# Attention scores over the full 128 rows, and the order of every engine written down block by block

## The chip, the cores and the metric

The kernel runs on one core of one Trainium2 chip. The metric is device time in microseconds, taken over a whole execution of the program; the times given are medians over several executions, and lower is better. A core has five engines with a queue each: PE (TensorE, matrix products; PEld is its loading of weights), DVE (VectorE), ACT (ScalarE), POOL (GpSimd) and SP (SyncE, which issues transfers). Each takes its own queue in order, and they wait for one another by semaphores.

## The reference

One inference step of a two-layer network. 128 context tokens ("prompt") and 512 noisy tokens on an 8 by 64 grid ("sample") pass through an even layer (a pooling mixer beside a neighbourhood attention) and an odd layer (convolutions). The change lies in the even layer's attention, with 8 heads of 64:

```python
s_loc = jnp.einsum('brqhd,brkwhd->bhrqkw', qg, k_band).astype(jnp.float32) * scale + bias
s_loc = jnp.where(col_ok[:, None, :], s_loc, -jnp.inf)
s_ctx = jnp.einsum('brqhd,bhld->bhrql', qg, kc).astype(jnp.float32) * scale
s = jnp.concatenate([s_loc.reshape(bsz, N_HEADS_B, rows, GRID_W, n_loc), s_ctx], axis=-1)
p = jax.nn.softmax(s, axis=-1).astype(v.dtype)
...
o = (jnp.einsum('bhrqkw,brkwhd->brqhd', p_loc, v_band)
     + jnp.einsum('bhrql,bhld->brqhd', p_ctx, vc))
```

Every sample query sees a band of 16 columns over all 8 rows, with a learned bias by relative position, and 128 cached context keys, in one softmax. The prompt's queries see the prompt's keys (`context_attention`, a plain softmax). Then the attention is gated by silu(g_b), and it goes with the pooling mixer through one output projection. Beside it, layer modulation needs `silu(cond) @ w_mod`, 3 by 1024 columns for each layer and for two conditions.

## The kernel before

Activations lie with channels on the 128 partitions and 640 tokens along the free dimension: 256 of the sample, 128 of the prompt, 256 of the sample. A projection takes a weight tile of 1024 by 128 (512 KB) and makes 128 output channels. Each float32 operand is split into a high part that the fast matmul takes exactly and a low rest (`split`: ACT copies the high part, DVE subtracts), and three products hi hi, hi lo and lo hi are added up in PSUM. `mm_k` issues the six matmuls of one slice of 128 input channels (three products, 384 and 256 tokens each); eight of them make one tile (`mtile`). Weight tiles come in the order of the list `order`; `next_w` and `ahead` load and split them up to two tiles ahead, from the queue of ACT.

The attention stage follows the projection to v (L532). For each of four pairs of heads (`attention(i)`) it projects k, then q, and splits both. The two heads of a pair lie on partitions 0 to 63 and 64 to 127. A block is 128 queries (8 columns by 8 rows, two groups of 8 columns; the edges form the fourth block) by 384 keys. For each of four blocks `scores` issues six matmuls: three products for each head, each over the 64 rows of that head (L587). Then `softmax`: DVE adds the bias and takes the minimum of the negated sum out of PSUM (L593), ACT makes the exponential and its sum (L596), DVE the reciprocal (L598) and the normalised row (L599). `flip` transposes the result on PE (L605) and ACT copies it out (L607); `values` multiplies by v (L617) into the bank `ps_o`. The prompt has its own scores (L628) and values (L651). Last come the gating (L675 to L682) and a split to `o_hi`, `o_lo`.

POOL builds the bias of each head out of `raw_b` (`build_bias`: L450 adds a mask, L452 copies, L454 makes two edge parts); `raw_b` holds all eight heads and is loaded from SP in 16 transfers (L518) during the pooling mixer. The rest of the modulation, 32 rows of 1024 columns in `todo`, is made on DVE: `fill_mod(n)` takes n rows, each with two products over 1024 elements (L260), and `dma_wt` issues the row for the next fill from SP (L251), with two buffers `wt`. How many rows are filled where is set by `FILL`, `FILL_P`, `FILL_V` and `FILL_O`. Two output tiles (`early`) are projected at the end of the stage.

What sets the order: in most of the program a planner places the instructions by its own costs and due times. `keep_in_program_order` ties one instruction to its place, `chain` ties the attention's matmuls to one another, and inside `manual_schedule(engines=...)` the engines named follow the order of the code; before, only the start of the program is written so. PSUM has eight banks: two tiles `mm` of two banks, two of `ps_s`, one each of `ps_t` and `ps_o`.

## Time and profile before

| | |
|---|---|
| time, median of 3 runs | 594.07 us (593.48 to 594.58) |
| span of the profiled execution, first to last instruction | 592.7 us |
| a time of its own for the profiled execution | not given; the median lies 1.4 us above its span |
| PE busy | 580.5 us, 98% |
| DVE busy | 444.2 us, 75% |
| ACT busy | 224.2 us, 38% |
| POOL busy | 39.1 us, 7% |
| granted TensorE clock, mean | 0.997 |

The profile lists one execution. A row of the order of time gives start and duration in us, engine, line, operation, output and inputs, shape and count, and in square brackets the idle time ahead of it with what ended that. A group row gives busy us, mean ns of one, and idle time before. Matmuls are pipelined: what one costs is the time from its start to the next one's start, not its duration. The chain of waits is followed back from the last instruction to whatever released each one.

### The profile page before, as it was taken

What the parts mean: (1) busy time and instruction counts of PE and PEld (TensorE: products, weight loads), DVE (VectorE), ACT (ScalarE), POOL (GpSimd) and SP (SyncE); (2) the same over time, 40 slices, a digit from 0 to 9 for tenths busy, and PEclk for the clock granted to TensorE, in tenths of its full rate; (3) what the DMA queues carried; (4) which work ended last, traced back from release to release, by engine and by line L of the source; (5) the groups of instructions that cost most, each with busy time, mean ns of one, the idle gap of its engine ahead of it and who ended that gap; (6) DMA issues with size and microseconds to landing.
All of it is one profiled execution on the core that took longest, in us unless ns stands there. A gap on an engine that the chain in (4) does not pass through costs nothing.

```text
span 592.7 us, 10405 instructions
## 1 busy us (share of the span) xinstructions
PE 580.5 (98%) x4218; PEld 538.7 (91%) x4218; DVE 444.2 (75%) x802; ACT 224.2 (38%) x392; POOL 39.1 (7%) x89
## 2 busy tenths in 40 slices
PE   9799999999999999999999999999999999999995
PEld 5699999988988788878999999999999999999994
DVE  0566577698979879775638889999999995457536
ACT  6557222223354555464325431123222222445220
POOL 1000000330004223100000000000000000000000
PEclk9999999999999999999999999999999999999998
DMA  8985566556833333311811232222222222110204
GB/s 306 373 361 173 175 177 173 149 191 204 270 96 128 108 111 102 118 71 43 273 41 37 72 115 88 83 72 72 72 71 72 74 84 91 53 57 2 72 0 178
DMA packets 24991, 74.21 MB, mean 125 GB/s; under 512 B 2800, under 2 KB 7024, under 8 KB 24816
## 3 DMA queue, kind: packets, MB, share of 16 engines
q1 hardware_dynamic: 15584, 39.86, 20.0%
q10 hardware_dynamic: 9360, 33.69, 17.2%
q8 instruction: 33, 0.54, 0.4%
q14 instruction: 14, 0.11, 0.1%
HBM read 70.39 MB, written 3.15 MB: 124 GB/s over the span
## 4 chain that ended last, share of the span: by engine, by line
PE 96%; DMA 1%; DVE 1%; ACT 0%; issue 0%; POOL 0%; DVEq 0%; SPq 0%; ACTq 0%; POOLq 0%
PE mm L162 77%; PE ps_o L617 3%; PE ps_s L587 3%; PE ps_t L605 3%; PE ps_s L532 2%; PE mm L301 2%; PE modacc L324 1%; DMA wm<-in_w_mod 1%; PE ps_t L532 1%; PE ps_o L532 1%; PE mm L532 1%; PE bc L200 1%; PE mm L494 1%; PE modtr L192 1%; PE stat L192 0%; DVE y L957 0%
## 5 line engine op out<-in xcount | busy, mean ns | idle before, releaser
L162 PE MATMUL mm<-h_lo,w_hi 128*128 128x384 f32 (+1 forms) x768 | 181.1, 311 | 0.5 <-DVE h_lo L345 0.5
L162 PE MATMUL mm<-h_hi,w_hi 128*128 128x384 f32 (+1 forms) x768 | 181.3, 313 | 0.0
L162 PE MATMUL mm<-h_hi,w_lo 128*128 128x384 f32 (+1 forms) x768 | 181.2, 311 | 0.0
L112 ACT CAST w_hi<-w_raw 128x1024 fp32r<-128x1024 f32 x68 | 70.9, 1054 | 162.9 <-PE mm L162 142.0
L162 PEld LDWEIGHTS mm<-h_hi,w_hi 128*128 128x128 f32 x768 | 119.1, 188 | 3.3 <-issue 2.1
L162 PEld LDWEIGHTS mm<-h_lo,w_hi 128*128 128x128 f32 x768 | 119.4, 188 | 2.5 <-issue 1.4
L162 PEld LDWEIGHTS mm<-h_hi,w_lo 128*128 128x128 f32 x768 | 119.5, 188 | 1.1 <-issue 1.1
L910 DVE SCALAR_TENSOR_TENSOR cv<-gl,small,cv 128x656 f32<-128x656 f32 x120 | 101.5, 901 | 0.4
L115 DVE TENSOR_TENSOR w_lo<-w_raw,w_hi 128x1024 fp32r<-128x1024 f32 x68 | 83.5, 1230 | 15.7 <-ACT w_hi L112 15.6
L260 DVE SCALAR_TENSOR_TENSOR junk<-wt,condb 128x1024 bf16<-128x1024 f32 x64 | 78.6, 1229 | 5.5 <-DMA wt<-in_w_modT 4.8
L162 PE MATMUL mm<-o_lo,w_hi 128*128 128x384 f32 (+1 forms) x256 | 67.8, 312 | 0.0
L162 PE MATMUL mm<-o_hi,w_lo 128*128 128x384 f32 (+1 forms) x256 | 67.7, 311 | 0.0
L162 PE MATMUL mm<-o_hi,w_hi 128*128 128x384 f32 (+1 forms) x256 | 66.7, 313 | 0.0
L162 PEld LDWEIGHTS mm<-o_hi,w_hi 128*128 128x128 f32 x256 | 43.0, 189 | 1.0 <-issue 0.6
L162 PEld LDWEIGHTS mm<-o_lo,w_hi 128*128 128x128 f32 x256 | 43.2, 189 | 0.8 <-issue 0.3
L162 PEld LDWEIGHTS mm<-o_hi,w_lo 128*128 128x128 f32 x256 | 43.2, 189 | 0.7 <-issue 0.5
L607 ACT COPY pt<-ps_t 128x384 f32<-128x384 f32 (+1 forms) x36 | 16.7, 464 | 24.4 <-PE ps_t L605 24.2
L596 ACT ACTIVATE sn<-sn,mx 128x384 f32<-128x384 f32 x32 | 19.6, 615 | 12.6 <-DVE mx L593 11.6
L593 DVE CUSTOM_DVE_ANT_0 sn<-ps_s,bias 128x384 f32<-128x384 f32 x32 | 17.2, 551 | 5.4 <-PE ps_s L587 5.3
L733 DVE SCALAR_TENSOR_TENSOR x<-mm,mod,x 128x128 f32<-128x128 f32 (+2 forms) x19 | 8.5, 494 | 14.8 <-PE mm L162 14.8
L733 DVE SCALAR_TENSOR_TENSOR x<-mm,mod,xre 128x128 f32<-128x128 f32 (+2 forms) x19 | 8.6, 493 | 14.3 <-PE mm L162 14.3
L605 PE MATMUL ps_t<-ident,sn 128*128 128x128 f32 x104 | 18.6, 285 | 0.5 <-ACT pt L607 0.3
(199 smaller groups left out, 601.4 us busy)
## 6 DMA issues: line engine op xcount, KB each, us to landing
wt<-in_w_modT SPq DMA_DIRECT2D x32, 512.0 KB, 4.2
w_raw<-in_w_in_odd ACTq DMA_DIRECT2D x28, 512.0 KB, 3.4
wm<-in_w_mod SPq DMA_DIRECT2D x16, 512.0 KB, 8.9
w_raw<-in_w_in_even ACTq DMA_DIRECT2D x16, 512.0 KB, 4.0
w_raw<-in_w_out_even ACTq DMA_DIRECT2D x8, 512.0 KB, 5.3
w_raw<-in_w_out_odd ACTq DMA_DIRECT2D x8, 512.0 KB, 3.4
x<-in_xT SPq DMA_DIRECT2D x8, 320.0 KB, 6.5
xre<-in_xN SPq DMA_DIRECT2D x8, 320.0 KB
```

Source lines behind the costliest of these rows:

```text
L112: op = S.copy(hi, src)
L115: V.tensor_tensor(lo, src, hi.bitcast(F32), op=ALU.subtract)
L162: PE.matmul(ps[:, PB + t0:PB + t1], ww[:, ks], xx[k][:, t0:t1], start=(first and i == 0), stop=(last and i == 2))
L260: tc.keep_in_program_order(V.scalar_tensor_tensor(junk, wt, 1.0, condb[:, c, :], op0=ALU.mult, op1=ALU.mult, accum_out=mod[l][:, j, d, c:c ...
L532: PE.matmul(vps[c], xx[k][:, vsl[c]], ww, start=(k == 0 and n == 0), stop=(k == NK - 1 and n == 2))
L587: chain(PE.matmul(sps[hh][:, 0:384], qq[hr, qs], km, start=(n == 0), stop=(n == 2)))
L593: V.tensor_tensor_reduce(out=sn, in0=sps[:, 0:384], in1=bs[hh][b], scale=-1.0, scalar=3e38, op0=ALU.add, op1=ALU.min, accum_out=mx)
L596: S.activation(sn, sn, AF.Exp, bias=mx, scale=-1.0, accum_out=sume)
L605: chain(PE.transpose(tps[:, c * P:(c + 1) * P], sn[:, c * P:(c + 1) * P], ident))
L617: chain(PE.matmul(po[hr, b * P:(b + 1) * P], vv, pts[hh][:, n * P:(n + 1) * P], start=(n == 0), stop=(n == 2)))
L733: V.scalar_tensor_tensor(o_, p_, g[:, c:c + 1], r_, op0=ALU.mult, op1=ALU.add)
L910: V.scalar_tensor_tensor(z, gl[i][:, w:w + TG], cd[:, i, w:w + 1], z, op0=ALU.mult, op1=ALU.add)
```

## The change

Scores go over 128 rows. For each head `qq` holds the high part of q on that head's 64 partitions and the low part on the other 64; `kh` holds the high part of k on both halves (one half copied by ACT, the other by a transfer from SP); `kl` holds the low part on the head's half and zeros on the other. So two matmuls for each head make the three products. The normalisation moves from DVE to POOL (`norm`). The next pair's `k_lo` comes behind the last scores of a pair, since there is one `kl`.

The whole stage stands in `manual_schedule` for all five engines. `stream` is a generator of projection slices (q before k, then the last gate, then seven slices of each early output tile), and `feed(n)` emits n of them. After 22 slices come 16 steps, one for each block: scores, slices, normalisation, the flips of the block before, one modulation row, slices, the values of the block before, slices; `STEPS` says how many slices stand at the three places. In the second step of a pair the prompt scores follow the scores. Prompt flips, prompt values and the second head's flips now use the banks of `ps_s`. Weight tiles are loaded from SP (`prefetch`, two raw tiles ahead of the two split ones). `raw_b` holds two heads, and `load_raw` loads the next pair's, in 16 transfers from SP, in the fourth step of pairs 0 and 1, behind `bias_edge`; the first pair's is loaded in the pooling mixer and the second's ahead of the steps. The host lays `cache_k` out twice.

```diff
-FILL = ((1, 1, 2), (2, 0, 1), (1, 1, 1), (1, 2, 2))
-FILL_P, FILL_V, FILL_O = (2, 1, 1, 1, 1, 1, 0, 1, 0), (2, 2, 2, 2), (2, 2, 2, 2, 2, 2, 2)
+FILL_P, FILL_V, FILL_O = (2, 1, 1, 1, 1, 1, 0, 1, 0), (2, 2, 2, 2), (1, 1, 1)
...
+STEPS = ((1, 2, 1), (1, 2, 1), (1, 2, 1), (1, 2, 1)) + ((1, 2, 1), (1, 2, 1), (1, 2, 1), (1, 1, 1)) * 2
+STEPS += ((1, 1, 1), (1, 1, 0), (1, 1, 0), (1, 1, 1))
...
-    order += [a["w_in_even"][m + i] for i in range(4) for m in (12, 8)] + [a["w_in_even"][23]]
+    order += [a["w_in_even"][m + i] for i in range(4) for m in (8, 12)] + [a["w_in_even"][23]]
...
-    ready, live = [], []
+    ready, live, pre = [], [], []
+
+    def prefetch():
+        while order and len(pre) < 2:
+            pre.append(dma_w(order.pop(0), nc.sync))
 
     def ahead():
-        while order and len(live) + len(ready) < 4 and len(ready) < AHEAD:
-            ready.append(split_w(dma_w(order.pop(0))))
+        while (order or pre) and len(live) + len(ready) < 4 and len(ready) < AHEAD:
+            ready.append(split_w(pre.pop(0) if pre else dma_w(order.pop(0))))
...
-                tc.keep_in_program_order(V.scalar_tensor_tensor(
-                    junk, wt, 1.0, condb[:, c, :], op0=ALU.mult, op1=ALU.mult, accum_out=mod[l][:, j, d, c:c + 1]))
+                op = V.scalar_tensor_tensor(junk, wt, 1.0, condb[:, c, :], op0=ALU.mult, op1=ALU.mult,
+                                            accum_out=mod[l][:, j, d, c:c + 1])
+                if not by_hand:
+                    tc.keep_in_program_order(op)
...
-    raw_b = att.tile([P, NH, 256], F32, name="raw_b", bufs=1)
...
+    def load_raw(i):
+        t = att.tile([P, 2, 256], F32, name="raw_b", bufs=1)
+        for r in range(8):
+            for m in range(2):
+                p0 = 64 * m + 8 * r
+                nc.sync.dma_start(t[p0:p0 + 8], bass.AP(
+                    tensor=rf.tensor, offset=rf.offset + 2 * i * RBW + 31 * r + 8 * m + 24,
+                    ap=[[1, 8], [RBW, 2], [1, 256]]))
+        raw_b[:] = [t]
+
+    bs = [[t[:, 128:512], t[:, 512:896], t[:, 0:384], t[:, 896:1280]] for t in bias]
+
+    def bias_inner(j):
+        t = bias[j]
...
+
+    def bias_edge(j):
         for s in range(2):
...
-        for r in range(2 * g, 2 * g + 2):
-            for m in range(2):
-                p0 = 64 * m + 8 * r
-                nc.sync.dma_start(raw_b[p0:p0 + 8], bass.AP(
-                    tensor=rf.tensor, offset=rf.offset + 31 * r + 8 * m + 24, ap=[[1, 8], [RBW, NH], [1, 256]]))
+        if g == 1:
+            load_raw(0)
...
+    kl = atp.tile([P, 2, T], F32R, name="kl", bufs=1)
+    for hh in range(2):
+        G.memset(kl[HR[1 - hh], hh, :].bitcast(F32), 0.0)
+
+    def ctx_in(i):
+        cs = atp.tile([P, 2, P], F32, name="ctxk", bufs=1)
+        nc.sync.dma_start(cs, a["cache_k"][:, i])
+        st_[i]["cs"] = cs
+    def k_in(i, ps):
+        kh = atp.tile([P, 2, T], F32R, name="kh")
...
+        for hh in range(2):
+            hr, ot = HR[hh], HR[1 - hh]
+            S.copy(tok_sample(kh[hr, hh, :]), ps_sample(ps[hr]))
+            nc.sync.dma_start(tok_sample(kh[ot, hh, :]).bitcast(F32), tok_sample(kh[hr, hh, :]).bitcast(F32))
+        S.copy(kh[:, :, 256:384], st_[i]["cs"])
         S.copy(k32, ps_prompt(ps))
         nc.sync.dma_start(a["out_k"][i], k32)
+        st_[i].update(kh=kh, kps=ps, k32=k32)
+
+    def k_lo(i):
+        kh, ps, cs = (st_[i][n] for n in ("kh", "kps", "cs"))
+        for hh in range(2):
+            hr = HR[hh]
+            V.tensor_tensor(tok_sample(kl[hr, hh, :]), ps_sample(ps[hr]), tok_sample(kh[hr, hh, :]).bitcast(F32),
+                            op=ALU.subtract)
+        for hh in range(2):
+            hr = HR[hh]
+            V.tensor_tensor(kl[hr, hh, 256:384], cs[hr, hh], kh[hr, hh, 256:384].bitcast(F32), op=ALU.subtract)
...
+    def q_in(i, ps):
+        qq = atp.tile([P, 2, TS], F32R, name="qq")
+        q32 = atp.tile([P, TP], F32, name="q32")
+        pieces = [(hh, slice(o, o + 2 * n), view(ps[HR[hh]], PB + off, [[step, 2], [1, n]]), n)
+                  for hh in range(2) for o, off, step, n in ((0, 64, 320, 192), (384, 0, 576, 64))]
+        for hh, qs, src, n in pieces:
+            S.activation(two(qq[HR[hh], hh, qs], n), src, AF.Copy, scale=0.125)
+        S.activation(q32, ps_prompt(ps), AF.Copy, scale=0.125)
+        for hh, qs, src, n in pieces:
+            V.scalar_tensor_tensor(two(qq[HR[1 - hh], hh, qs], n), src, 0.125, two(qq[HR[hh], hh, qs].bitcast(F32), n),
                                    op0=ALU.mult, op1=ALU.subtract)
+        st_[i].update(qq=qq, q32=q32, pts={}, sns={})
...
-        def scores(b):
-            qs = slice(64 + 128 * b, 192 + 128 * b) if b < 3 else slice(512, 640)
-            sps = [ps_s.tile([P, 512], F32, name="ps_s") for _ in range(2)]
-            for n, (qq, kk) in enumerate(((qh, kh), (ql, kh), (qh, kl))):
-                for hh in range(2):
-                    hr = slice(64 * hh, 64 * hh + 64)
-                    km = kk[hr, 128 * b:128 * b + 384] if b < 3 else view(kk[hr, :], 0, [[256, 3], [1, 128]])
-                    chain(PE.matmul(sps[hh][:, 0:384], qq[hr, qs], km, start=(n == 0), stop=(n == 2)))
-            return [softmax(b, hh, sps[hh]) for hh in range(2)]
...
+    def scores(i, b):
+        c = st_[i]
+        sps = [ps_s.tile([P, 512], F32, name="ps_s") for _ in range(2)]
+        for hh in range(2):
+            qv = c["qq"][:, hh, 128 * b:128 * b + 128]
+            for n, kk in enumerate((c["kh"], kl)):
+                km = kk[:, hh, 128 * b:128 * b + 384] if b < 3 else view(kk[:, hh, :], 0, [[256, 3], [1, 128]])
+                PE.matmul(sps[hh][:, 0:384], qv, km, start=(n == 0), stop=(n == 1))
...
+    def norm(i, b):
+        for sn, sume in st_[i]["sns"][b]:
+            rc = atp.tile([P, 1], F32, name="rc", bufs=4)
             V.reciprocal(rc, sume)
-            V.tensor_scalar(sn, sn, rc, None, op0=ALU.mult)
+            G.tensor_scalar(sn, sn, rc, None, op0=ALU.mult)
...
+        spp = [ps_s.tile([P, 512], F32, name="ps_s") for _ in range(2)]
+        for hh in range(2):
+            PE.matmul(spp[hh][:, 0:P], c["q32"][HR[hh]], c["k32"][HR[hh]], start=True, stop=True)
...
+    def flip(pool, sn, n, name="pt"):
+        tps = pool.tile([P, 512], F32, name=pool.name)
+        for k in range(n):
+            PE.transpose(tps[:, k * P:(k + 1) * P], sn[:, k * P:(k + 1) * P], ident)
+        pt = atp.tile([P, n * P], F32, name=name, bufs=2 if n == 3 else 1)
+        S.copy(pt, tps[:, 0:n * P])
+        return pt
...
+    def values_prompt(i):
+        c = st_[i]
+        pop = ps_s.tile([P, 512], F32, name="ps_s")
...
     early = []
-    for n in range(2):
+    def stream():
+        for i in range(4):
+            for take in (q_in, k_in):
+                w = next_w(len(live))
+                prefetch()
+                if take is k_in:
+                    ctx_in(i)
+                ps = pmm.tile([P, 1024], F32, name="mm")
+                for k in range(NK):
+                    mm_k(ps, w, h_hi, h_lo, k, k == 0, k == NK - 1)
+                    if k < NK - 1:
...
+                take(i, ps)
+                yield
...
+    with tc.manual_schedule(engines={ET.PE, ET.Activation, ET.DVE, ET.Pool, ET.SP}):
+        by_hand.append(1)
+        work = stream()
+        def feed(n):
+            for _ in range(n):
+                if next(work, StopIteration) is StopIteration:
+                    return
+
+        def flips(n):
+            i, b = divmod(n, 4)
+            c = st_[i]
+            if b == 1:
+                c["ptp"] = flip(ps_s, c["snp"], 2, "ptp")
+            c["pts"][b] = [flip(pool, sn, 3) for pool, (sn, _) in zip((ps_t, ps_s), c["sns"][b])]
+        def outs(n):
+            i, b = divmod(n, 4)
+            if b == 1:
+                values_prompt(i)
+            values(i, b)
+            if b == 3:
+                gate_b(i)
+        for j in range(2):
+            bias_inner(j)
+            bias_edge(j)
+        feed(16)
+        load_raw(1)
+        k_lo(0)
+        feed(6)
+        for n in range(16):
+            i, b = divmod(n, 4)
+            scores(i, b)
+            if b == 3 and i < 3:
+                k_lo(i + 1)
+            if b == 1:
+                prompt_scores(i)
+            feed(STEPS[n][0])
+            norm(i, b)
+            if i < 3 and b == 2:
+                bias_inner(0)
+                bias_inner(1)
+            if i < 3 and b == 3:
+                bias_edge(0)
+                bias_edge(1)
+                if i < 2:
+                    load_raw(i + 2)
+            if n:
+                flips(n - 1)
+            fill_mod(1)
+            feed(STEPS[n][1])
+            if n:
+                outs(n - 1)
+            feed(STEPS[n][2])
+        feed(1)
+        flips(15)
+        feed(2)
+        outs(15)
+        feed(99)
+        for w, ps in early:
+            mm_k(ps, w, o_hi, o_lo, NK - 1, False, True)
+        early = [ps for _, ps in early]
+    by_hand.clear()
...
-            fill_mod(FILL_O[2 + m])
+            if l == 0 and m < len(FILL_O):
+                fill_mod(FILL_O[m])
...
-        A["cache_k"][0, 0].transpose(0, 2, 1).reshape(4, P, P).transpose(1, 0, 2))
+        np.repeat(A["cache_k"][0, 0].transpose(0, 2, 1).reshape(4, 2, 1, HD, P), 2, axis=2).reshape(4, 2, P, P)
+        .transpose(2, 0, 1, 3))
```

188 lines of the change are left out of this document (76 added, 112 removed).

## The prediction, made before the change was run

> **What bounds the kernel now.** The page comes first: how busy the engines are, and which of them the chain that ended last runs through.
>
> ```profile
> span 592.7 us, 10405 instructions
> PE 580.5 (98%) x4218; PEld 538.7 (91%) x4218; DVE 444.2 (75%) x802; ACT 224.2 (38%) x392; POOL 39.1 (7%) x89
> PE 96%; DMA 1%; DVE 1%; ACT 0%; issue 0%; POOL 0%; DVEq 0%; SPq 0%; ACTq 0%; POOLq 0%
> ```
>
> PE holds 96% of the chain, so the change is worth what it takes from PE's queue, less what PE is made to wait. All of it lies in one stage, whose ends I take from PE's order of time: its first row is the first matmul behind the v projection, its last the one behind the two output tiles that are begun early.
>
> ```profile
> 142.15 0.45 PE L162 MATMUL mm<-h_hi,w_hi 128*128 128x384 f32 x2
> ...
> 276.62 0.46 PE L162 MATMUL mm<-o_hi,w_hi 128*128 128x384 f32 x2
> ```
>
> The stage takes 276.62 - 142.15 = 134.5 us. The chain of waits inside it shows what PE pays for:
>
> ```profile
> 46.93 35.31 PE mm L162 x240
> 160.96 0.42 PE ps_s L628 x4
> 161.38 4.30 PE mm L162 x28
> 165.68 0.37 PE ps_s L587
> 166.06 0.49 PE mm L162 x2
> 166.54 0.72 PE ps_s L587 x5
> ...
> 170.08 0.37 PE ps_t L651 x4
> ...
> 178.53 0.33 PE ps_t L605 x3
> ...
> 180.26 0.81 PE ps_o L617 x12
> ```
>
> The first row is the undisturbed rate: 240 matmuls in 35.31 us, 0.294 us for a pair of 384 and 256 columns, so 0.176 for 384. A lone score matmul of 64 rows (165.68) takes 0.37, and the two wide ones behind it 0.49 in place of 0.29: PE pays when it changes between the full array and half of it. The order of time prices one change:
>
> ```profile
> 165.34 0.34 PE L162 MATMUL mm<-h_hi,w_lo 128*128 128x384 f32 x1
> 165.61 0.44 PE L587 MATMUL ps_s<-kh,qh 64*128 64x384 f32 x1
> ```
>
> From start to start 0.27, against 0.176: 0.09 for each change. In the stage's order of time, from its first row to its last, the shape changes 106 times, about 9.8 us.
>
> **Step 1, PE's own list.** For the new stage, each line a count by a row above: 11 weight tiles of 24 pairs by 0.294 = 77.6 (unchanged). Scores: 16 blocks by 4 matmuls of the full 128 rows by 0.176 = 11.3; before, six half ones, 0.72 in one piece and more when torn. Flips: 32 of 0.33, and four of two transposes, 0.22 each = 11.4. Values 16 by 0.81 = 13.0. Prompt scores and prompt values, eight groups of 0.42 or 0.37 = 3.2. Changes of the array's shape: only values (in and out, 32) and prompt scores (8) are left, 40 by 0.09 = 3.6. Sum 120.1: 14.4 us less than 134.5, if PE waits for nothing. Of this 90 lie in the 16 steps (56 blocks of six matmuls, 49.4, and the rest), 19.4 ahead of them (22 such blocks) and 10.5 behind.
>
> The Trainium skill, TensorEngine Tiling (Array Packing), Performance Considerations, wants a contraction of 64 or less run as two row tiles side by side; by that alone the change loses 16 by (4 - 3) by 0.176 = 2.8 us. Its Key Properties say that a change of tiling mode drains the array, which the 0.27 against 0.176 agrees with; with it the sum is the 120.1 above.
>
> **Step 2, DVE's written order.** So far instructions pass each other as they become ready. Now each engine's queue is as written: in a step DVE does two masked minima, waits for the exponentials, does two reciprocals, then the two modulation products (the fill), then what the fed projection asks, and only then the next step's minima. Its rows, the stage first (length, then busy time of PE, PEld, DVE, ACT and POOL), then groups of it, then single instructions (start, duration):
>
> ```profile
> 142.30:276.60 134.30, 133.81 (x953) 111.84 (x952) 107.64 (x286) 66.72 (x163) 23.90 (x24) 1.00 0.37 120
> ```
>
> ```profile
> L599 DVE TENSOR_SCALAR sn<-sn,rc 128x384 f32<-128x384 f32 x32 | 14.0, 449 | 0.2
> L115 DVE TENSOR_TENSOR w_lo<-w_raw,w_hi 128x1024 fp32r<-128x1024 f32 x10 | 12.3, 1229 | 0.8 <-ACT w_hi L112 0.8
> L566 DVE TENSOR_TENSOR kl<-mm,kh 128x512 fp32r<-128x512 f32 x4 | 2.8, 690 | 2.0 <-ACT k L565 1.8
> L673 ACT ACT_TABLE_LOAD x1 | 1.3, 1283 | 0.0
> ```
>
> ```profile
> 197.03 0.56 DVE L593 CUSTOM_DVE_ANT_0 sn<-ps_s,bias 128x384 f32<-128x384 f32 x1 [1.10 <-PE ps_s L587]
> 197.52 0.55 DVE L593 CUSTOM_DVE_ANT_0 sn<-ps_s,bias 128x384 f32<-128x384 f32 x1
> 203.62 1.22 DVE L260 SCALAR_TENSOR_TENSOR junk<-wt,condb 128x1024 bf16<-128x1024 f32 x1
> 204.77 0.08 DVE L260 DVE_READ_ACCUMULATOR junk<-wt,condb 128x1 f32 x1
> 215.98 0.41 DVE L679 TENSOR_TENSOR bo<-ps_o,gb 128x96 f32<-128x96 f32 x2
> 217.58 0.82 DVE L115 TENSOR_TENSOR o_lo<-bo,o_hi 128x640 fp32r<-128x640 f32 x1
> ```
>
> ```profile
> 198.34 0.60 ACT L596 ACTIVATE sn<-sn,mx 128x384 f32<-128x384 f32 x1
> 198.84 0.19 ACT L596 ACTIVATION_READ_ACCUMULATOR sn<-sn,mx 128x1 f32 x1
> ```
>
> The change takes the 14.0 us of L599 from DVE (to POOL); k's low part becomes two half-height instructions of each size, as long as the whole ones. A group of four steps then asks of DVE: minima 8 by 0.49 = 3.9; reciprocals 0.8; products 8 by 1.15 (start to read-out) and some lock = 9.4; k low 1.6; q low 1.4, by k's rate; two weight splits 2.4; prompt softmax 1.2; gating 1.9, by L679 and L115. That is 22.6 of work. To it come waits that nothing fills in a fixed order: the second exponential is read out at 199.03, 2.0 after the first minimum, against 0.98 of minima, so 1.0 in three of four steps (k low covers the fourth), 0.9 at the prompt, and 0.9 while ACT makes o_hi. Sum 27.4. PE's list for the same group (15 fed blocks) is 23.8. For the four groups DVE needs 24.5 (no gating), 27.4, 27.4 and 24.1 (no q or k, one split), 103.4 against PE's 90: 13 us. PE can't run ahead: ps_s has two banks, the second flip of a step takes the bank that this step's first minimum must free, and the prompt scores take both. Bounds: nothing, if those banks leave room, and 18, if I lay the steps one behind another with no give. I take 15, for the groups are uneven and a step in which PE is late gives nothing back. ACT is at 66.7 of 134.3 and has room; two more loads of its table (1.28 each) fall in DVE's lateness.
>
> **Step 3, SP's written order.** SP now issues the weights too, and in steps 3 and 7 of the 16 the relative-bias load (16 small DMAs) stands ahead of the DMA that brings the next step's modulation row. That load overwrites raw_b, so its first DMA waits for POOL's last edge of the bias, and SP waits with everything behind it.
>
> ```profile
> 180.40 0.40 POOL L452 COPY bias<-bias 128x256 f32<-128x256 f32 x1
> ...
> 232.40 1.28 POOL L452 COPY bias<-bias 128x256 f32<-128x256 f32 x1
> ...
> 236.59 3.44 POOL L454 TENSOR_SCALAR bias<-raw_b,small 128x128 f32<-128x128 f32 x4 [0.79 <-DVE mx L593]
> ```
>
> ```profile
> wt<-in_w_modT SPq DMA_DIRECT2D x32, 512.0 KB, 4.2
> ...
> ctxk<-in_cache_k SPq DMA_DIRECT2D x4, 64.0 KB, 1.8
> ```
>
> ```profile
> 105.70 1.52 SPq L518 DMA_DIRECT2D raw_b<-in_rpb  x4
> ```
>
> ```profile
> SPq L251 <- DVE junk L260: 119.6, 25, 15.0
> ```
>
> ```profile
> DVE junk L260 <- DMA wt<-in_w_modT: 4.8, 4, 1.9
> ```
>
> The row of SP's own waits shows that its queue stands still at one (15.0 us at most); now other transfers stand behind. The last row is what DVE waited for modulation rows so far, 4.8 us in the whole run. From the first minimum of step 3: minima and k low 2.6, normalisation until 4.7, four edge instructions 3.4 to 4.4 (8.5), 16 issues by 0.38 (14.6), landing 4.2 (18.8). DVE wants that row one step (5.9) and 2.0 later, at 8: it stands about 10 us, between 9 (faster landing) and 13 (slow POOL). Behind the waiting product stand the gating and the next minima, and PE stops at the prompt scores of step 5 for their banks. Two such places: 20 us. The third and fourth bias loads are the only ones in the steps; the first two come earlier and cost nothing.
>
> Of POOL's normalisation (128x384) no row exists: the copy, 0.40 for 256, gives 0.6; L454, 3.44 for four of 128, gives 2.6. I take 0.7, nearest to the copy, whose run is unbroken too. The copy of 1.28 had a modulation product beside it. The Trainium skill, SBUF — State Buffer, Who interferes with whom, says that a DVE instruction with two SBUF inputs and a GpSimd one that reads SBUF shut each other out; 1.28 against 0.40 agrees, and without it each bias load would start 1 us earlier, 2 in all.
>
> Costs at nothing: the two copies of k's halves by DMA (1.8 by ctxk's landing) are covered by the six fed blocks (5.3) ahead of step 0 and by a step later; uncovered they cost about 2 each, 8. Weight loads behind SP's wait have two tiles of slack, 14 us; beyond that they would hold a tile back.
>
> **Sum.** 120.1 + 15 + 20 = 155.1, against 134.5: 20.6 more. The profiled execution has span 592.7, so 613.3; the median of the runs lies 1.4 above that span (594.07), which gives 614.7.
>
> **Rivals.** *SP holds back, DVE else keeps pace* (PE's list is what counts, and products fit into its gaps): 120.1 + 1 + 18 = 139, time 599. For it: DVE was idle 27 of 134 us and lost 14 of work. *DVE's order alone*, the rows arrive in time: 135.1, time 595. For it: DVE waited 4.8 us in all for wt. *The other side*: the written order does not bind DVE and SP as strictly as I read it. Its place is the fill between reciprocals and next minima; it decides if the next minima start within PE's step of 5.9. Then both waits go at once, and the list counts: 120 to 124, time 580 to 584, by how far the banks of ps_s still bind (0 to 4, one prompt wait of 1 in each group). Against it: the diff names DVE and SP among the engines whose order is fixed. *POOL is the bound*, at 2.6 a normalisation: 32 by 2.6 and 24 of bias is 107, past PE's 90, and both loads start 4 later: 630. *Full height brings nothing*, halves were cheap: the list is 2.8 above before, 597, and the 0.37 of a lone half matmul speaks against it.
>
> **How the numbers follow.** Chances: 0.48 for the forecast (own range 605 to 624), 0.17 for SP alone, 0.10 for DVE's order alone (half of it no worse than before), 0.18 for the other side, 0.04 for POOL, 0.03 for no gain. Within 0.2% (1.2 us) is what this kernel's measurement can't tell from no change. Faster: 0.18 and a third of DVE's order, 0.21; within 0.2%: 0.04; slower 0.75. The range goes from 580, the lower end of the other side, to 624, where DVE's order costs 18 and each hold-back 13; POOL and the ends of the cases, some 0.15, are left out.
>
> **What would show it.** Step 1: L587 at 0.176 from start to start, no 64-row score matmuls, about 40 changes of shape. Step 2: PE idle ahead of the flips and the prompt scores with DVE's minima as releaser. Step 3: DVE standing about 10 us twice at L260 for wt, SP's raw_b issues behind a POOL wait just before it. The prediction is wrong if L260 hardly waits for wt, or if PE's rows in the stage show no gap above 1 us.

## The result and the profile after

The changed kernel takes 633.64 us (median, 631.52 to 636.63) against 593.89 us: 1.0673 times as long, 95% interval 1.0641 to 1.0704. The forecast was 615, with 580 to 624 as its range: the direction came true, the size was 18.6 us too small.

The page of the changed kernel (span, busy time, granted clock in 40 slices, chain of waits by engine):

```profile
span 632.1 us, 10457 instructions
PE 580.4 (92%) x4186; PEld 549.5 (87%) x4186; DVE 446.4 (71%) x786; ACT 227.1 (36%) x404; POOL 85.5 (14%) x123
...
PEclk9999999999988597698999999999999999999998
...
PE 75%; DVE 9%; DMA 5%; issue 4%; ACT 2%; POOL 2%; SPq 2%; DVEq 0%; POOLq 0%
```

PE no longer holds the chain alone (96% before, 75% now), and in the attention stage the granted clock falls to 0.5. The order of time shows the stage's ends, a block of scores, the longest but one of PE's stops, and what led to it on SP and DVE:

```profile
141.98 0.45 PE L168 MATMUL mm<-h_hi,w_hi 128*128 128x384 f32 x2
...
161.34 0.34 PE L617 MATMUL ps_s<-kh,qq 128*128 128x384 f32 x1
161.51 0.33 PE L617 MATMUL ps_s<-kl,qq 128*128 128x384 f32 x1
...
171.08 1.27 PE L643 MATMUL ps_s<-k,q 64*128 64x128 f32 x4 [4.67 <-DVE mx L622]
...
196.91 5.42 SPq L460 DMA_DIRECT2D raw_b<-in_rpb  x16
202.37 0.83 SPq L258 DMA_DIRECT2D wt<-in_w_modT  x2
...
205.89 1.23 DVE L267 SCALAR_TENSOR_TENSOR junk<-wt,condb 128x1024 bf16<-128x1024 f32 x1 [10.31 <-DMA wt<-in_w_modT]
...
213.95 0.55 DVE L622 CUSTOM_DVE_ANT_0 sn<-ps_s,bias 128x384 f32<-128x384 f32 x1
...
214.57 1.27 PE L643 MATMUL ps_s<-k,q 64*128 64x128 f32 x4 [15.08 <-DVE mx L622]
...
316.03 0.45 PE L168 MATMUL mm<-o_hi,w_hi 128*128 128x384 f32 x2
```

The stage takes 316.03 - 141.98 = 174.05 us, 39.6 more than before; the rest of the span is 458.1 us against 458.2, so all of it lies here. The last rows are one story: SP issues 16 transfers of the bias, then the modulation row; DVE stands 10.31 us for that row; the minima behind it start at 213.95; and PE, whose prompt scores need the banks that the minima free, stands for 15 us.

The waits (total, number, longest) name the same two, and SP's own:

```profile
PE ps_s L643 <- DVE mx L622: 37.8, 4, 15.2
DVE junk L267 <- DMA wt<-in_w_modT: 23.2, 4, 10.3
SPq L460 <- POOL bias L476: 17.6, 2, 8.8
```

What the forecast had left out shows in stretches around that stop (length, busy time of PE, PEld, DVE, ACT and POOL, then the granted clock):

```profile
198.60:201.00 2.40, 0.89 (x6) 0.56 (x4) 0.00 (x0) 0.00 (x0) 0.73 (x1) 1.00 0.19 50
...
205.00:209.00 4.00, 0.00 (x0) 0.00 (x0) 3.06 (x6) 0.00 (x0) 0.00 (x0) 0.50 0.37 149
...
214.60:218.00 3.40, 3.40 (x13) 3.18 (x14) 1.87 (x10) 2.06 (x8) 0.00 (x0) 0.50 0.46 166
218.00:222.00 4.00, 4.00 (x33) 3.63 (x32) 2.62 (x5) 0.96 (x2) 3.63 (x2) 0.93 0.09 17
```

PE stands, the clock halves, and it stays halved for 4 us after PE has work again: two matmuls of a projection, 384 and 256 columns, take 0.53 us from start to start there (217.00 to 217.53) and 0.29 at full speed (219.60 to 219.89). The clock's records give four such stretches in the stage, 6.8, 17.1, 17.1 and 3.4 us long.

From PE's rows the stage is taken apart for each kernel below: *waits* are the distances from start to start above 0.45 us, less 0.2; *half speed* is half of PE's time at clock 0.5; *list* is what is left.

| kernel | time, us | stage | list | waits | half speed |
|---|---|---|---|---|---|
| before | 593.9 | 134.5 | 134.0 | 0.5 | 0 |
| after | 633.6 | 174.1 | 120.8 | 43.6 | 9.7 |
| row first | 612.2 | 153.3 | 120.5 | 22.9 | 9.9 |
| norm on ACT | 627.4 | 168.7 | 118.3 | 32.9 | 17.5 |
| scores alone | 601.7 | 141.8 | 127.1 | 11.4 | 3.3 |
| gate later | 609.5 | 150.3 | 121.2 | 21.1 | 8.0 |
| third step, fewer products | 606.7 | 145.4 | 119.8 | 20.8 | 4.8 |
| last pair free | 604.2 | 144.2 | 120.6 | 20.6 | 3.0 |
| ahead of the split | 603.9 | 144.5 | 122.1 | 19.1 | 3.2 |
| third product out | 604.5 | 139.8 | 122.2 | 14.2 | 3.4 |

### The profile page after: what moved, and what is told of

It reads as the page before. It is cut to its first block, busy times and chain, and to the rows that moved or that the text cites. A ratio compares the mean times of both kernels' runs of the same rounds, so it can differ in the third digit from the quotient of the medians.

```text
span 632.1 us, 10457 instructions
## 1 busy us (share of the span) xinstructions
PE 580.4 (92%) x4186; PEld 549.5 (87%) x4186; DVE 446.4 (71%) x786; ACT 227.1 (36%) x404; POOL 85.5 (14%) x123
## 3 DMA queue, kind: packets, MB, share of 16 engines
q10 hardware_dynamic: 7488, 26.87, 13.1%
## 4 chain that ended last, share of the span: by engine, by line
PE 75%; DVE 9%; DMA 5%; issue 4%; ACT 2%; POOL 2%; SPq 2%; DVEq 0%; POOLq 0%
PE mm L168 65%; DMA wt<-in_w_modT 3%; DVE junk L267 3%; PE mm L310 2%; SPq L460 2%; PE ps_o L671 1%; DVE w_lo L117 1%; POOL sn L633 1%; PE modacc L333 1%; PE ps_s L617 1%; DVE sn L622 1%; DVE qq L606 1%; DMA wm<-in_w_mod 1%; PE ps_s L657 1%; PE ps_s L643 1%
## 5 line engine op out<-in xcount | busy, mean ns | idle before, releaser
L168 PE MATMUL mm<-h_hi,w_hi 128*128 128x384 f32 (+1 forms) x768 | 183.6, 318 | 0.0
L168 PEld LDWEIGHTS mm<-h_hi,w_hi 128*128 128x128 f32 x768 | 120.5, 190 | 4.9 <-issue 3.9
L267 DVE SCALAR_TENSOR_TENSOR junk<-wt,condb 128x1024 bf16<-128x1024 f32 x64 | 82.7, 1292 | 25.7 <-DMA wt<-in_w_modT 24.7
L168 PE MATMUL mm<-o_hi,w_lo 128*128 128x256 f32 (+1 forms) x256 | 67.0, 311 | 0.0
L633 POOL TENSOR_SCALAR sn<-sn,rc 128x384 f32<-128x384 f32 x32 | 49.5, 1557 | 102.4 <-DVE rc L632 91.6
L643 PE MATMUL ps_s<-k,q 64*128 64x128 f32 x16 | 4.8, 454 | 37.8 <-DVE mx L622 37.8
L643 PEld LDWEIGHTS ps_s<-k,q 64*128 64x128 f32 x16 | 3.5, 277 | 39.3 <-DVE mx L622 39.3
```

Source lines behind the costliest of these rows:

```text
L168: PE.matmul(ps[:, PB + t0:PB + t1], ww[:, ks], xx[k][:, t0:t1], start=(first and i == 0), stop=(last and i == 2))
L267: op = V.scalar_tensor_tensor(junk, wt, 1.0, condb[:, c, :], op0=ALU.mult, op1=ALU.mult, accum_out=mod[l][:, j, d, c:c + 1])
L633: G.tensor_scalar(sn, sn, rc, None, op0=ALU.mult)
L643: PE.matmul(spp[hh][:, 0:P], c["q32"][HR[hh]], c["k32"][HR[hh]], start=True, stop=True)
```

## The experiments

**The written order of SP.** *Row first*: the bias load goes behind the fill, and with it behind the modulation row.

```diff
-                if i < 2:
-                    load_raw(i + 2)
             if n:
                 flips(n - 1)
             fill_mod(1)
+            if i < 2 and b == 3:
+                load_raw(i + 2)
```

> The changed kernel, with one move: the transfers of the next pair's bias are issued behind the modulation row of the step, not ahead of it. Theory (SP's written order holds DVE back, 10.3 us twice, and PE stands for it at the prompt scores of steps 5 and 9): the two waits of L267 for wt go, the stalls of 15.4 and 15.6 us at the prompt scores shrink to about 5 each, as at step 1; 633.6 - 20.6 = 613, and down to 608 if the half clock behind the stalls becomes shorter too. Rival (DVE is full anyway, the hold-back lies in time that it would have needed): 630 to 634. Second rival (the wait only moves on, to the row of the step after): 620 to 628.

612.2 us, ratio 1.0307 (1.0291 to 1.0322). Its waits:

```profile
PE ps_s L643 <- DVE mx L622: 17.0, 4, 5.4
...
DVE junk L267 <- DMA wt<-in_w_modT: 2.9, 2, 2.2
```

DVE's waits for the rows go from 23.2 to 2.9 us, PE's waits fall by 20.7, the time by 21.4. The hold-back is shown, and its size too. Half speed stays at 9.9, for a stop of 5 us is followed by as much of it as one of 15.

*Four loads*: the order of the changed kernel, the load in 4 transfers.

```diff
-        for r in range(8):
-            for m in range(2):
-                ...
+        for m in range(2):
+            for hh in range(2):
+                nc.sync.dma_start(t[64 * m:64 * m + 64, hh], ...)
```

> The changed kernel, with each pair's bias loaded by 4 transfers of 64 partitions in place of 16 of 8; place and wait unchanged. Theory (the hold-back is POOL's part plus SP's issues, 0.34 us each, one behind another): 12 issues fewer, so SP reaches the modulation row 4.1 us sooner, twice: 633.6 - 8.2 = 625.4, between 623 and 628. Rival (SP's wait for POOL's last edge is all of it, the issues overlap): 632 to 635.

629.67 us, 1.0606 (1.059 to 1.0622): 4 us less, some half of what was expected. Four larger transfers take SP 2.65 us to issue, 0.66 each where a small one takes 0.34, so only some 2.8 us are saved at each place; DVE's longest wait for a row falls from 10.3 to 8.3. The issues are the smaller part of the hold-back; what SP stands for is POOL's bias (17.6 us in 2).

*Norm on ACT*: the normalisation leaves POOL for ACT, and SP's order stays.

```diff
-            G.tensor_scalar(sn, sn, rc, None, op0=ALU.mult)
+            S.activation(sn, sn, AF.Copy, scale=rc)
```

> The changed kernel, with the normalisation on ACT (a scaled copy) in place of POOL. Theory (POOL's 1.2 to 1.8 us for each normalisation stand ahead of the bias's edges and so of the bias load, and the modulation products beside them take 1.48 us in place of 1.15): the edges end about 3 us sooner, so each hold-back falls from 10.3 to about 7, and DVE saves 0.3 us in a step: 633.6 - 6 - 5 = 622, between 618 and 627. Rival (POOL is off every path that counts): 632 to 635. Second rival (ACT becomes late for the exponentials): over 636.

627.36 us, 1.0555 (1.053 to 1.058).

```profile
PE ps_s L643 <- DVE mx L622: 15.8, 4, 5.5
...
PE ps_o L671 <- ACT pt L659: 10.5, 6, 2.8
...
DVE junk L267 <- DMA wt<-in_w_modT: 3.8, 4, 1.3
```

With POOL free the bias is ready early and the hold-back goes (3.8 us), the order of SP unchanged: the chain is POOL's normalisation, then its bias, then SP's load, then the row. But ACT's copies of the transposes are late now (10.5 us), and half speed grows to 17.5. The price of the normalisation on POOL, from the groups of the changed kernel:

```profile
L633 POOL TENSOR_SCALAR sn<-sn,rc 128x384 f32<-128x384 f32 x32 | 49.5, 1557 | 102.4 <-DVE rc L632 91.6 <-PE ps_t L657 10.7
```

1.56 us each, twice the 0.7 taken.

**The clock.** *Warm*: PE gets matmuls of no use (36, 120, 120 and 20, with 256 columns) ahead of the prompt scores, so that it does not stand.

```diff
+                wps = ps_t.tile([P, 512], F32, name="ps_t")
+                for _ in range((36, 120, 120, 20)[i]):
+                    PE.matmul(wps[:, 0:256], warm[:, 0:P], warm, start=True, stop=True)
```

> The changed kernel, with small matmuls that nobody reads (36, 120, 120 and 20 of 256 columns in bf16) put into PE's queue ahead of the four prompt scores, into the time in which PE stands still. No wait is taken away. Theory (each stall of 3 us and more halves PE's clock for what follows: 44 us at half clock in the records, 9.7 us of PE's work in the stage at twice its time): granted clock back to 0.99 and above, time 633.6 - 9.7 = 624, between 622 and 627. Rival (the lower clock falls into idle time alone): 633 or a little more, since PE has more to do.

628.63 us, 1.0585 (1.0556 to 1.0614), 5 us less with the hold-backs untouched:

```profile
DVE junk L267 <- DMA wt<-in_w_modT: 22.9, 4, 10.1
...
PE ps_s L643 <- DVE mx L622: 4.4, 3, 2.1
```

The four stops keep their length with the filler in them: from the scores ahead to the prompt scores they take 37.5 us, where the changed kernel has 38.3, and PE still waits 0.1 to 2.1 us behind the filler. Half speed falls from 9.7 to 1.7, of which 5 us arrive in the time. Some of the rest goes to PE's later wait for ACT's copies at L671 (0.7 to 2.2 us); where the remainder went was not followed. That half speed is a cost of its own, beside the waits, is shown. The Trainium skill, TensorE: Matmul & The Clock Gate, Part 1 (What's actually happening), says that the array falls to half its clock after an idle window of about 3.4 us and comes back after a busy one; the stretches of 3.4, 6.8 and 17.1 us agree, as multiples of 3.41. The length of the idle time does not agree everywhere: in *third product out*, below, a stop of 2.41 us (166.94 to 169.35) is followed by 3.41 us at half speed (from 169.44), with PE busy for 1.3 of the 3.4 us ahead of it.

**The scores alone.** The kernel before, its planner kept, with the 128-row scores (and the bias load by pairs, normalisation on DVE).

```diff
-                    km = kk[hr, 128 * b:128 * b + 384] ...
-                    chain(PE.matmul(sps[hh][:, 0:384], qq[hr, qs], km, start=(n == 0), stop=(n == 2)))
+                km = kk[:, hh, 128 * b:128 * b + 384] ...
+                chain(PE.matmul(sps[hh][:, 0:384], qv, km, start=(n == 0), stop=(n == 1)))
```

> The kernel before, in the planner's order, with one part of the change alone: scores over the full 128 rows (q's parts stacked, k's high part on both halves by a transfer, k's low part padded with zeros, one buffer of it), and the bias loaded pair by pair to make room. Theory (the half-height scores cost PE their changes of shape, about 0.09 us each, and lone halves): changes of shape fall from 106 to about 50, PE's list by 8 to 14 us; some of it lost to the transfers of k's halves: 584 to 589. Rival (the planner already hides it, or the transfer of k's halves comes on the path): 593 to 600.

601.71 us, 1.014 (1.0119 to 1.016): a gain was expected, a loss came. The list does shrink, by 6.9 us, and the shape changes from 106 to 62. But 11.4 us of waits and 3.3 of half speed appear. The waits are spread over ACT's copies, DVE's reciprocals and minima, none above 2.8 us. A shorter list on PE was worth nothing here, where what PE waits for kept its length.

**Amount or order of DVE's work.** All that follow have the modulation row ahead of the bias load, as *row first* has (612.2), to learn what its 22.9 us of waits are. *Quarter* makes each modulation product over 256 of its 1024 columns (the modulation is then incomplete).

> The run with the row first (612.2), but the modulation products in the 16 steps go over 256 of the 1024 columns, so that three quarters of these sums are left out; count, order and transfers as they are. 32 instructions of about 0.35 us in place of 1.15: 25.6 us less on DVE. Theory (the products stand ahead of the next minima in DVE's queue, and PE's 22.9 us of waiting and 9.9 us of half clock in the stage follow from that): PE's list is left, with 1 or 2 us of waits for the banks: 580 to 587. Rival (the waits belong to the chain minima, exponentials, banks, whatever DVE has to do): 598 and more.

608.92 us, 1.0247 (1.0228 to 1.0267). DVE's busy time in the stage falls from 110 to 83 us, the time by 3, and most of the wait is still there:

```profile
PE ps_s L644 <- DVE mx L623: 13.9, 4, 5.4
```

At step 5, PE's second stop, DVE's order of time in *quarter* shows why:

```profile
193.65 1.53 DVE L607 SCALAR_TENSOR_TENSOR qq<-mm,qq 64x384 fp32r<-64x384 f32 x4 [1.30 <-ACT q L605]
195.21 1.23 DVE L117 TENSOR_TENSOR w_lo<-w_raw,w_hi 128x1024 fp32r<-128x1024 f32 x1
...
198.45 0.82 DVE L117 TENSOR_TENSOR o_lo<-bo,o_hi 128x640 fp32r<-128x640 f32 x1 [0.79 <-ACT o_hi L114]
199.19 0.55 DVE L623 CUSTOM_DVE_ANT_0 sn<-ps_s,bias 128x384 f32<-128x384 f32 x1
```

The shorter products leave DVE idle for 1.30 us until ACT has q; then q's low half, the weight's low half and the gating stand ahead of the minima, 5.5 us of them. The amount of the products is not the cause. Two ways to move the products missed as well. *Fill early* puts the fill ahead of the reciprocals:

> The changed kernel, with the step's modulation row moved on DVE from behind the flips to ahead of the reciprocals, into the time in which DVE waits for the exponentials (its transfer is thereby issued ahead of the bias load too, as in the run with the row first, 612.2). Theory (a fixed order leaves 1.0 us empty on DVE in some nine of the 16 steps, and DVE's lateness is what PE waits for at the prompt scores): 612.2 less 5 to 9, and a few us of half clock: 602, between 597 and 607. Rival (it is DVE's work as such; the empty time counts nothing): 610 to 614. Second rival (the reciprocals come later, and so the normalised rows on POOL, and flips wait): over 614.

619.45 us, 1.0425 (1.0404 to 1.0446): the second rival; the reciprocals came later, and the flips waited for POOL (7.1 us, 1.3 in *row first*) and the values for ACT (2.2, from 0.8). *Fewer fills* drops the fill from the first step of each pair (four rows go to the output projection), puts those of the second and third ahead of the reciprocals, and the prompt scores behind the first slice:

> A version meant to beat both, with the scores and the hand-written order of the changed kernel: no modulation row in the first step of a pair (four rows go to the output projection, where DVE has room), in the second and third it stands in the wait for the exponentials, in the fourth ahead of the bias load; the prompt scores come behind the first fed slices, with their normalisation split off. Theory (DVE then needs about 22 us for each four steps, PE's list 23.8, so PE's list sets the time): stage 121 to 127 us, time 581 to 588. Rival (PE still waits for single banks, as behind the scores alone in the planner's order): 592 to 604.

610.71 us, 1.0282 (1.0263 to 1.0301): prompt scores 10.6, but the prompt's flips now 5.4 in 4.

**Moving what waits.** *Prompt later*: the prompt scores behind the second portion of slices. *Gate later*: `gate_b(i - 1)` from the end of a pair's first step to behind the reciprocals of its second. *Both*.

```diff
-            if b == 1:
-                prompt_scores(i)
             feed(STEPS[n][0])
...
             feed(STEPS[n][1])
+            if b == 1:
+                prompt_scores(i)
```

```diff
-            if b == 3:
+            if n == 15:
                 gate_b(i)
...
                 flips(n - 1)
+            if b == 1 and i:
+                gate_b(i - 1)
             fill_mod(1)
```

> Built on the kernel with the modulation row ahead of the bias load (612.2 us). The prompt scores of a pair no longer stand directly behind the block scores whose banks they take: they come behind the second portion of the stream, so PE has about 6 us of products and transposes between the two. Theory (PE stands because the prompt scores ask for a bank that DVE has not yet read, and it has other work that could go first): 17.6 us of waits at the prompt scores fall to about 3; the transposes of the step, which take the next bank, inherit some 1.5 us at each of steps 5 and 9; the half-speed stretches behind the stalls (9.9 us) fall to about 4. Sum 612.2 - 14.6 + 3 - 6 = about 594.6, range 590 to 600. Rival (DVE is behind at that place by its amount of work, and whichever instruction next needs a bank waits as long): the waits move to the transposes nearly whole, 608 to 612.

> Built on the same kernel (612.2 us). The gating of a pair's output (five multiplications and the low half, about 2.8 us of DVE, of which 0.8 is a wait for ACT's high half) moves from the end of the first step of the next pair to behind the minima and the reciprocals of its second step. Theory (the wait at the prompt scores is the burst q low half, weight low half, gating that stands ahead of the minima): the stalls of steps 5, 9 and 13 shorten by about 2.8, 2.8 and 2 us, and with them the half-speed stretches by about 3 us: 612.2 - 7.6 - 3 = about 601.6, range 598 to 605. Rival (the value products of that second step, which need the one output bank that the gating reads, now wait for it instead): 610 to 615.

> Built on the same kernel (612.2 us), with both edits: prompt scores behind the second portion of the stream, gating behind the reciprocals of the second step. Theory: the minima come in time and nothing waits for a bank at steps 1, 5, 9 and 13; of the 17.6 us of waits there about 2 are left, of the 9.9 us of half speed about 3: 612.2 - 15.6 - 7 = about 589.6, range 586 to 595, that is near or below the kernel before (593.9). Rival (the two edits take away the same wait, so the sum is no better than the better of them): no more than 2 us below the better one, 593 to 600. Second rival (DVE is behind by its amount of work): 605 to 612.

610.0 (1.0278, 1.0236 to 1.032), 609.48 (1.0262, 1.0224 to 1.03) and 614.16 us (1.0341, 1.0309 to 1.0373): all three theories missed. With both, the prompt scores wait no more, and others do:

```profile
PE ps_s L617 <- ACT snp L647: 13.4, 4, 4.8
PE ps_s L657 <- DVE mx L622: 5.0, 3, 2.7
```

By the written order the prompt scores hold their banks until ACT has read them, their maxima stand behind the gating and the fill, and the next block's scores pay. *Third step* therefore moves the prompt scores, their flips and values one step on (`b == 2` for `b == 1`); *third step, fewer products* also drops the fill of each pair's first step (`if b:` ahead of `fill_mod(1)`, `FILL_O` one entry longer).

> Built on the kernel with the modulation row ahead of the bias load and the gating behind the reciprocals of the second step (609.5 us). The prompt scores move on to the third step of the pair, behind the second portion of the stream, where DVE stood idle for some 2 us; their transposes and value products follow one step later. Theory (bunching: steps 1, 5, 9 hold q's low half, a weight's low half, prompt softmax and gating together, about 10 us of DVE in a step of 7 us of PE): of the 21 us of waits about 8 are left and of the 8 us of half speed about 3: 609.5 - 13 - 5 = about 591, range 587 to 598. Rival (two score banks and the chain minima, exponential, normalisation, transposes are short in every step, and a wait removed here comes back in the next): 605 to 612.

> The same, and the modulation product of each pair's first step (2.6 us of DVE, four of them) moves to the output projection's first tiles. Theory: the minima of steps 5, 9 and 13 come before PE asks for their bank, 3 to 5 us less of waits and 1 to 2 of half speed than in the kernel with the third step alone: about 586, range 583 to 593, faster than the kernel before (593.9). Rival (the products fill DVE's idle time anyway): the same as the kernel with the third step alone, within 1.5 us. Second rival: the four products delay the output projection's first tiles by their 10 us, 596 to 602.

611.68 (1.0287, 1.0263 to 1.0311) and 606.65 us (1.021, 1.0186 to 1.0235). The 5 us between the two were expected, the level was not: the rival held for the third step. With the load in 4 transfers in addition:

> The same as the kernel with four products fewer, and each bias load of a pair as four larger transfers in place of 16. Theory (with the modulation row ahead of it the load is behind nothing that PE waits for, so its issues cost nothing): the same within 1 us. Rival (the weight rows issued behind it are late by the 4 us of the issues): 1 to 4 us less.

608.64 us, 1.0253 (1.022 to 1.0285); the intervals overlap and both spans are 603.3: once the row is ahead, the issues cost nothing. Then the prompt's maxima ahead of that step's fill, and on top of it the last pair's three rows (of two products each) to the output projection:

> Built on the kernel with the prompt scores in the third step and four products fewer (606.7 us). On DVE the maxima of the prompt scores go ahead of that step's modulation product, and the prompt's normalisation behind it. Theory (the wait of the fourth step's scores for the prompt's exponential, 8.3 us in 4, is the product's 2.6 us ahead of the maxima): that wait falls to about 1, half speed from 4.8 to 3: 606.7 - 7 - 2 = about 598, range 595 to 601. Rival (the bank comes free earlier but the product now delays the minima of the fourth step, and its transposes wait): 603 to 608.

> The same, and the three modulation products of the last pair move to the output projection's first tiles too. Theory (the waits of the last pair, about 8 us, are DVE's products between short portions of the stream): 4 to 5 us less than the kernel with the maxima first, about 593.5, range 590 to 598, within 1% of the kernel before. Rival (the last pair waits for its own chain of exponential, normalisation and transposes, with too little of the stream left to cover it): the same as the kernel with the maxima first, within 1.5 us.

608.74 (1.0245, 1.022 to 1.027) and 604.15 us (1.0177, 1.015 to 1.0203). The maxima ahead of the fill gained nothing, and the order of time of *last pair free* shows why:

```profile
206.59 1.19 ACT L580 CAST kh<-mm 64x512 fp32r<-64x512 f32 x2
206.97 0.49 PE L643 MATMUL ps_s<-k,q 64*128 64x128 f32 x4
...
207.80 0.40 ACT L582 CAST kh<-ctxk 128x256 fp32r<-128x256 f32 x1
208.23 0.27 ACT L583 COPY k<-mm 128x128 f32<-128x128 f32 x1
208.39 1.05 ACT L114 CAST w_hi<-w_raw 128x1024 fp32r<-128x1024 f32 x1
...
209.47 1.60 DVE L117 TENSOR_TENSOR w_lo<-w_raw,w_hi 128x1024 fp32r<-128x1024 f32 x1 [3.33 <-ACT w_hi L114]
211.00 0.47 DVE L644 TENSOR_REDUCE mx<-ps_s 128x1 f32<-128x128 f32 x2
...
211.71 0.37 ACT L647 ACTIVATE snp<-ps_s,mx 128x128 f32<-128x128 f32 x1 [2.27 <-DVE mx L645]
```

The prompt scores start at 206.97. DVE is idle for 3.33 us and does not take their maxima, for ahead of them in its order stands the low half of the next weight, which waits for ACT's high half, itself behind four copies of k. And with the row of the stage (it reaches 4.5 us past its end)

```profile
142.00:290.00 148.00, 129.08 (x948) 119.06 (x947) 94.60 (x250) 72.22 (x180) 60.51 (x56) 0.98 0.35 112
```

DVE is busy for 94.6 of 148 us while PE waits for 20.6 in the stage. *Ahead of the split* puts the prompt scores between the two slices of the portion, so that the maxima precede that split:

```diff
-            feed(STEPS[n][1])
+            feed(STEPS[n][1] if b != 2 else 1)
             if b == 2:
                 prompt_scores(i)
+                feed(STEPS[n][1] - 1)
```

> Built on the kernel with the last pair's products moved (604.2 us). In the third step of a pair the prompt scores stand between the two portions of the stream, not behind both: on DVE their maxima then come ahead of the low half of the next weight, which waits for ACT. Theory (DVE's written order puts an instruction that waits for ACT ahead of one that could run): of the waits of the fourth step's scores (5.4 us) and of the prompt's transposes (5.1 us) at most 2 are left, half speed falls by 1: 604.2 - 8.5 - 1 = about 594.7, range 592 to 598. Rival (the wait is for want of a third bank: the next instruction that takes one waits as long): 602 to 606.

603.87 us, 1.0156 (1.0127 to 1.0186):

```profile
PE ps_s L661 <- DVE mx L622: 13.1, 8, 3.3
...
PE ps_s L617 <- ACT snp L647: 0.5, 1, 0.5
```

```profile
209.44 0.29 DVE L644 TENSOR_REDUCE mx<-ps_s 128x1 f32<-128x128 f32 x1 [0.37 <-PE ps_s L643]
...
212.35 1.36 DVE L117 TENSOR_TENSOR w_lo<-w_raw,w_hi 128x1024 fp32r<-128x1024 f32 x1 [2.42 <-ACT w_hi L114]
213.63 1.22 DVE L267 SCALAR_TENSOR_TENSOR junk<-wt,condb 128x1024 bf16<-128x1024 f32 x1
...
216.58 0.55 DVE L622 CUSTOM_DVE_ANT_0 sn<-ps_s,bias 128x384 f32<-128x384 f32 x1
```

The wait that was aimed at is gone (5.7 to 0.5), the maxima follow the prompt scores at once (209.44); but the split still waits 2.42, the fill stands behind it, and the minima at 216.58 are what the flips wait for (9.7 to 13.1). So the last one takes that fill out of the third step too (three rows more to the output projection):

> Built on the kernel with the prompt's maxima ahead of the split (603.9 us). The three modulation products left in the third steps (2.5 us of DVE each) move to the output projection's first tiles, where DVE has room. Theory (written order: the minima of the fourth step stand behind that product, which itself stands behind the split that waits for ACT): the waits of the transposes of the prompt fall from 8.6 us to about 2, half speed from 3.2 to 2, 603.9 - 6.6 - 1.2 = about 596, range 594 to 599. Rival (the wait comes back at the next instruction that takes a score bank): 601 to 604.

604.5 us, 1.016 (1.0135 to 1.0185). The stage does get 4.7 us shorter, with waits of 14.2; the time stays, for the output projection is that much longer. Its stretch in *third product out*, and PE's stops in it:

```profile
142.00:281.35 139.35, 126.41 (x919) 116.05 (x918) 83.15 (x228) 70.25 (x178) 57.00 (x56) 0.98 0.32 102
281.35:325.00 43.65, 40.60 (x280) 39.40 (x279) 42.25 (x74) 11.71 (x16) 0.72 (x15) 1.00 0.62 203
```

```profile
313.22 0.45 PE L168 MATMUL mm<-o_hi,w_lo 128*128 128x384 f32 x1 [1.92 <-DVE w_lo L117]
...
318.45 0.38 PE L168 MATMUL mm<-o_hi,w_hi 128*128 128x256 f32 x1 [1.13 <-DVE x L855]
```

DVE is busy for 42.25 of 43.65 us there: seven rows found room, ten do not, and PE loses 4.7 us outside the stage (462.8 us against 458.1). No version came below the kernel before; the best in the written order is 1.6% above it, the scores alone in the planner's order 1.4%.

## Why the prediction was wrong

The sum was 120.1 + 15 + 20 = 155.1 for the stage; it took 174.05.

- *Step 1, PE's list*: right. 120.8 for 120.1; score rows 0.17 apart, 40 shape changes. Across all the experiments with the new order it stays between 118 and 122.
- *Step 3, SP's order*: the mechanism was right. DVE stood 10 us twice for a row, behind POOL and the 16 issues; taking the load out of the row's way gave 21.4 us where 20 stood. That the size fits so well is in part luck, as these rows of the changed kernel show beside those of SP and DVE above:

```profile
187.55 0.55 DVE L622 CUSTOM_DVE_ANT_0 sn<-ps_s,bias 128x384 f32<-128x384 f32 x1
190.90 3.65 POOL L633 TENSOR_SCALAR sn<-sn,rc 128x384 f32<-128x384 f32 x2 [2.22 <-DVE rc L632]
194.53 2.35 POOL L476 TENSOR_SCALAR bias<-raw_b,small 128x128 f32<-128x128 f32 x4
```

  From the first minimum of step 3 (187.55) the normalisation ends at 7.0, where 4.7 was put, for POOL needs 1.8 us for each where 0.7 was taken. But the four edges take 2.35 where 3.4 to 4.4 were put, the issues 5.5 for 6.1 and the landing 3.5 for 4.2, so the row arrives at 18.3 where 18.8 was put: the errors cancel.
- *Step 2, DVE's written order*: this term failed. With the hold-back gone 22.9 us of waits are left where 15 were put, 7.9 too few; 17.0 of them stand at the prompt scores, with DVE's minima as releaser, as step 2 said. The method was at fault rather than a row: I summed DVE's work for a group of four steps and set it against PE's. Less work hardly helps (a quarter of the products: 3 us). What the rows show instead is which instruction stands first in the queue while it waits: q's low half and the weight's behind ACT, the gating and the low half behind `o_hi`, then the minima behind them. My list of waits in the group (1.0, 0.9, 0.9) lacks the one of the split for ACT's high half, 7.4 us in 5 in the stage of the changed kernel and 3.33 at once in the row of *last pair free*, though the group row of L115 quoted from before names that releaser, at 0.8 us in all.
- *The clock*: this term was put at nothing without a reason, and it is 9.7 us. I let PE stand for 35 us and counted standing only; behind each stop above 4 us in the runs of the table the clock is at half, and 4 to 6.6 us of work run at half speed.

The rest is 0.7 of list: 9.7 + 7.9 + 0.7 and 0.7 more of hold-back (20.7 for 20) make the 19 us. Of the rivals, *SP holds back, DVE else keeps pace* and *DVE's order alone* each drop a term that the runs show; *the other side* fell, as the written order binds DVE and SP strictly; *POOL is the bound* fell, although its price came out above my value: with 1.56 each it is busy 68.3 us of the 174. *Full height brings nothing* fell too: the list is 13.2 us shorter in the changed kernel and 6.9 with the scores alone.

Open is how much of the last 14 us of waits the eight banks impose. Following one wait at a time to the head of its queue, and moving ten rows out, shortened the stage from 153.3 to 139.8 us, each time with part of the wait coming back at the next instruction that takes a bank; no kernel with a third score bank was run, so banks and order aren't told apart to the end.

## What to carry to other kernels

When a planner's order is replaced by a written one, do not add up an engine's work: go through its queue and ask of each instruction what it waits for and who stands behind it. A shorter PE list was worth something here only as far as the chain beside it (minima, exponential, normalisation, transposes, copies, the loads behind them) got shorter too; and a stop of PE above some 4 us was to be priced here at its length plus 2 to 3.3 us for half speed, half of the 4 to 6.6 us measured. Work moved off a crowded stage goes where the engine has room by its row there: seven rows fitted into the output projection, and the three beyond them cost what they had saved.

## What the runs showed of the hardware

- After stops of 5.0 and 15.4 us PE's clock stays at half for 6.6 and 4.0 us more of work: the price hardly depends on the length of the stop (9.7 us in the stage with two stops of 15, 9.9 with stops of 4 to 6). Of stops of 2 to 3.6 us some brought a stretch of 3.4 us at half speed and some none: one of 2.41 us did in *third product out*, one of 3.54 us (213.65 to 217.19) did not in *ahead of the split*.
- POOL's `tensor_scalar` over 128x384 float32 takes 1.56 us on average, where DVE's took 0.449 before. Two in a row took 2.46 us with DVE idle (196.86 to 199.32) and 3.65 us beside DVE's modulation products and minima (190.90 to 194.53).
- 16 small transfers take SP 5.42 us to issue, 0.34 each, and four larger ones with the same data 2.65 us; in 4 transfers the time fell by 4 us, and by nothing once nobody waited behind them.
